# Driver counts, pairwise output transposes and the rank of the norm roots in a hybrid RWKV-7/S5 layer

## The chip, the core and the metric

The kernel runs on one core of a Trainium2 chip. The metric is the device time of one execution in microseconds (us); smaller is better. TensorE is called PE in the profile (PEld is its weight load), VectorE DVE, ScalarE ACT, GpSimd POOL and the SyncE queue SP.

## What is computed

One layer of a decoder trunk on x of 1 x 1024 x 1024 in float32, cut to what matters here:

```python
h = rms_norm(x, norm_mix_pre)
proj = h @ w_in                       # RWKV columns | S5 input u | two gates of 1024
o_rwkv = rwkv7_branch(...) @ w_branch_rwkv
o_s5   = s5_branch(...)    @ w_branch_s5
mixed = (sigmoid(gA) * o_rwkv + sigmoid(gB) * o_s5) @ w_out
x = x + rms_norm(mixed, norm_mix_post)
h = rms_norm(x, norm_ffn_pre)
x = x + rms_norm(conv_ffn(h, ...), norm_ffn_post)

# rwkv7_branch, per head of 64, for each time step t:
S = S * w_t + (S @ a_t) b_t^T + v_t k_t^T ;  y_t = S @ r_t
y = (y - mean) * rsqrt(var + 64e-5) * lnx_w + lnx_b      # per head
y = (y + sum(r * k * r_k) * v) * g
```

## The kernel before

The products are split: each float32 operand is a high part and a low part, and three matmuls of 128x512 stand for one (lines 171 to 175). One such triple is one *filler step*. Time is cut into two halves of 512 positions (`th` 0 and 1), the 512 RWKV channels into four blocks of 128, two per group `g`. The RWKV recurrence is solved in chunks of 64 steps: gram products (line 715), the inverse of triangular 32x32 blocks on DVE (`rwkv_inv`, lines 768 to 798: 30 pairs of multiply and add, in at 776 and out at 792 and 797 through DRAM), a level that joins the 32-blocks (`rwkv_level`, line 800), then eight chained chunks (`rwkv_chain`, line 855). `rwkv_out` (line 899) norms each head on DVE and ACT, transposes the result on PE (line 922), and multiplies it with the factors.

**Who sets PE's order.** PE's instructions stand in the order in which Python traces them. The middle of the kernel is traced by `drive` (lines 185 to 207). It holds *lanes*, generators whose steps yield a tuple of three: PE cost, how long until the lane may go on (or a condition), and optionally a weight. Beside them stands a list of *filler*: dense products, in a fixed order (gate tiles of the input projection, `merge`, `merge_s5`, `outproj`). `drive` has a clock `now` and a `credit`:

```python
if self.fill and self.credit < 0:
    continue                                   # no lane may step
...
self.now += r[0]
self.credit -= PACE * r[0] * (r[2] if len(r) > 2 else 1)      # PACE 0.8
lane[2] = r[1] if callable(r[1]) else self.now + r[1]
```

When no lane is due, or the credit is negative, one filler step is traced; it adds 0.68 to clock and credit, and the credit is capped at 2.0. So a lane step's second number is the planner's due time for the next step, and its cost times weight says how much filler must follow before another lane step. Lanes are tried in the order prep 0, prep 1, chain, output (line 1848). When the lanes are done, `drain` traces filler until `outproj` of half 0 is complete (line 1849); then `mix_out` goes on with `merge_rk`, which needs the split outputs of `rwkv_out` for half 1.

The steps of half 1 that matter:

- `chain_lane` (1878): `rwkv_nat` of group 0 (line 1882; transposes at 746 and 761 into natural layout, copied out by ACT at 753, 755 and 766), one wide piece of PE work with cost 2.0.
- `out_lane` (1893): `rwkv_out` of half 0, first pair due 32.0 (`T_LN`) after the chain of half 0. It takes both blocks of a group at once: eight transposes into two PSUM buffers `rp` (there are two in all), two ACT evictions (926), four DVE operations (934), and on SP four loads (933) and two stores `YR` (939). Two such steps, cost 1.0.
- `prep_lane` 1: the transposes of `kb` (701, two `rp` buffers, read by DVE at 703), two gram steps (715), the load for the inversion, `rwkv_nat` of group 1, then the inversion, which the driver counts as `T_INV` = 43.0 (line 1875) before the level may start.
- `rwkv_level`: block transposes on DVE (811) of what came back from DRAM (`gr`), then PE products (821, 831).
- after the chain of half 1, `rwkv_out` of half 1, first pair due `T_LE` = 20.0 later, factors loaded ahead; its squares lie in the three `ev` buffers (line 911), which the filler's gate loads (1184) use as well.

`merge_load` (1194) loads the four `YR` tiles; it is tried once from `merge_loads`, between two gate tiles of the filler, and does nothing while `outs` is under 2, that is until the output lane of half 0 is through; `merge` calls it again.

**Who sets the order on the other engines.** A list scheduler ranks instructions by priority: `high_priority(HPW)` (400000) for filler and weights, `HP2` (200000) for the prep and chain lanes and the middle norms, `HP` (100000) for the output lane, `HPN` (500000) for the start. Of what it counts as ready, the highest rank goes first; the order that results is fixed.

**Norm roots.** `rstd` (262) is one scaling and `rsqrt` (124): nine dependent small DVE operations, of which the last (139) releases `spread`, four PE transposes (271).

Of the kernel before, what the change touches and what calls it, by code (L numbers as in the profile page):

```python
# [12 lines left out]
AF = mybir.ActivationFunctionType  # L13
ALU = mybir.AluOpType
# [52 lines left out]
class Kern:  # L67
# [194 lines left out]
    def rstd(self, ss, eps, scale):  # L262

        v = self.small.tile([128, 4], F32, tag="rv", name=self.nm("rv"), bufs=2)
        self.nc.vector.tensor_scalar(v, ss[:, :4], scale, eps, ALU.mult, ALU.add)
        return self.rsqrt(v, 4, "nr")

    def spread(self, bc, y):

# [629 lines left out]
    def rwkv_out(self, ds, th, latency):  # L899

        nc, V, G, A = self.nc, self.nc.vector, self.nc.gpsimd, self.nc.scalar
        o = slice(th * 512, th * 512 + 512)
        for g in range(2):
            yn = self.yn[:, g].rearrange("p c u h i -> p (c u h) i")
            mean = self.small.tile([128, 16], F32, tag="lm", name=self.nm("lm"), bufs=2)
            V.tensor_reduce(mean, yn, AX.X, ALU.add)
            V.tensor_scalar(mean, mean, 1.0 / 64, None, ALU.mult)
            V.tensor_tensor(yn, yn, mean.unsqueeze(2).to_broadcast([128, 16, 64]), ALU.subtract)
            var = self.small.tile([128, 16], F32, tag="lv", name=self.nm("lv"), bufs=2)
            for j in range(2):  # L910
                sq = self.ev((128, 8, 64)) if th else self.tg("ld", NLD, (128, 8, 64))
                A.activation(sq, yn[:, 8 * j:8 * j + 8], AF.Square)
                V.tensor_reduce(var[:, 8 * j:8 * j + 8], sq, AX.X, ALU.add)
            V.tensor_scalar(var, var, 1.0 / 64, 64e-5, ALU.mult, ALU.add)
            y = self.rsqrt(var, 16, "or")
            V.tensor_tensor(yn, yn, y.unsqueeze(2).to_broadcast([128, 16, 64]), ALU.mult)
        yield 0, latency
        for g, d in enumerate(ds):
            ps = [self.rp((128, 4, 128)) for u in range(2)]
            for u in range(2):  # L920
                for c in range(4):
                    nc.tensor.transpose(ps[u][:, c], self.yn[:, g, c, u], self.cst("ident"))
            for u in range(2):
                p = 2 * g + u
                y1 = self.tg("ld", NLD)
                A.activation(y1, ps[u].rearrange("p c t -> p (c t)"), AF.Identity, bias=self.vec("lnx_b", p),
                             scale=self.vec("lnx_w", p))
                for src, op in ((d["bv"][u], ALU.add), (self.TG[p][:, o], ALU.mult)):
                    if th:
                        t = self.fac.pop(0)  # L930
                    else:
                        t = self.tg("ld", NLD)
                        nc.sync.dma_start(t, src)
                    V.tensor_tensor(y1, y1, t, op)
                if th:
                    self.brk.append(self.slots("eb", p))
                    self.split(*self.brk[p], y1)
                else:
                    nc.sync.dma_start(self.YR[p], y1)
            yield 1.0, 6.0 if th else 2.5  # L940


    def inproj(self, *jobs):
# [922 lines left out]
    def prep_lane(self, g):  # L1866
        for th in range(2):
            yield 0, (lambda: self.masked >= 2 * th + 1 and self.all_in) if g else (lambda: self.chunks >= 14 * th)
            d = self.ds[th][g]
            self.rwkv_tiles(d, g, th)  # L1870
            yield from self.rwkv_front(d, g, th, self.pts[th], (lambda: self.chains >= 1) if th > g else (lambda: self.grams > 2 * th) if g else T_LD)
            self.fronts += 1
            if g:
                yield from self.rwkv_inv(self.ds[th], th)
                yield 0, T_INV
                self.preps += 1

    def chain_lane(self):
        for th in range(2):
            ds = self.ds[th]  # L1880
            yield 0, lambda: self.fronts >= 2 * th + 1
            self.rwkv_nat(ds[0], 0)
            yield 2.0, lambda: self.preps > th
            yield from self.rwkv_level(ds)
            yield 0, lambda: self.outs >= 2 * th
            yield from self.rwkv_chain(ds, self.pts[th], th)
            if th:
                self.early_stack.close()
                self.early = self.early_stack.enter_context(self.tc.tile_pool(name="early", bufs=1, side="right"))
                self.chained = True  # L1890
            self.chains += 1
# [16 lines left out]
T_LD, T_SQ, T_LT = 6.0, 3.0, 3.5  # L1908
NEVA = 4
T_KN, T_BK, T_GR, T_NF, T_MT, T_INV, T_LV, T_CH = 7.0, 4.0, 4.0, 5.0, 8.0, 43.0, 1.0, 0.8  # L1910
T_LN, T_LE = 32.0, 20.0
T_N0, T_RS, T_N1, T_N2, T_N4, T_N5, T_N3 = 2.5, 4.0, 2.2, 5.0, 1.6, 40.0, 2.0
NET = 5
MGAP = 2
# [17 lines left out]
HPW, HPN = 400000, 500000  # L1932
# [64 lines left out]
```

## Time and profile before

| | us |
|---|---|
| three runs | 1499.52, 1508.82, 1509.49 (median 1508.82) |
| the profiled execution, own time | 1501.13 |
| its span, first to last instruction | 1499.4 |
| PE busy in the span | 1436.3 |
| DVE busy | 1072.2 |
| ACT busy | 730.3 |

Rows of the timeline read: start in us from the span's start, duration, engine, line, operation, output <- inputs, shape, count, and in brackets how long the engine was idle before and what released it. Rows of the waits read: who waited <- for whom: total us, times, longest. Rows of the windows read: stretch, its length, then busy time and instructions of PE, PEld, DVE, ACT and POOL, the granted PE clock (1.00 is full), the DMA share and GB/s.

### The profile page before, as it was taken

The numbers are of one execution on the slowest core, as the hardware profiler recorded it, in microseconds if no ns is written. First come the engines' busy times: TensorE is split into PE (matmuls) and PEld (weight loads), VectorE is DVE, ScalarE is ACT, GpSimd is POOL, SyncE is SP. The second block draws the span as 40 slices with busy tenths as digits, with TensorE's granted clock in tenths as the row PEclk, the third lists the DMA queues.
The fourth block names the chain that finished last, engine by engine and source line by source line (L and its number), as shares of the span: only waits on it lengthen the run. The fifth ranks groups of instructions, "written<-read, shape, count | busy, mean of one in ns | idle before, by whom it ended". The sixth has DMA issues, their size and how long they took to land. (4 is left out here: it accounts for less than half of the span.)

```text
span 1499.4 us, 24150 instructions
## 1 busy us (share of the span) xinstructions
PE 1436.3 (96%) x9284; PEld 1177.0 (78%) x9284; DVE 1072.2 (72%) x1761; ACT 730.3 (49%) x1167; POOL 58.7 (4%) x116
## 2 busy tenths in 40 slices
PE   7999999999999899798999999999999999999996
PEld 5778888788878687576878877888888887888785
DVE  8977774756226859456597799777777777697677
ACT  7677653533324564443455455444444444444351
POOL 0000000010100110100000000000000000000001
PEclk9999999999999999799999999999999999999997
DMA  6453432642512675433365633222222227943723
GB/s 221 124 187 113 131 94 93 203 133 100 170 52 76 189 222 177 135 100 113 117 197 179 204 125 128 84 79 78 83 85 84 85 71 243 322 143 126 229 95 112
DMA packets 121284, 206.26 MB, mean 138 GB/s; under 512 B 29248, under 2 KB 35520, under 8 KB 121168
## 3 DMA queue, kind: packets, MB, share of 16 engines
q1 hardware_dynamic: 113296, 182.43, 37.7%
q0 software_dynamic: 6144, 19.99, 4.0%
q10 hardware_dynamic: 1728, 2.29, 0.4%
q8 instruction: 73, 1.20, 0.3%
q14 instruction: 43, 0.35, 0.1%
HBM read 150.14 MB, written 52.43 MB: 135 GB/s over the span
## 5 line engine op out<-in xcount | busy, mean ns | idle before, releaser
L172 PE MATMUL gm<-hh,wh 128*128 128x512 f32 x672 | 276.6, 412 | 8.0 <-DVE rsy L139 5.1
L173 PE MATMUL gm<-hl,wh 128*128 128x512 f32 x672 | 265.7, 395 | 0.0
L174 PE MATMUL gm<-hh,wl 128*128 128x512 f32 x672 | 265.3, 395 | 0.0
L156 ACT CAST wh<-wf 128x512 fp32r<-128x512 f32 x171 | 105.7, 620 | 186.3 <-PE gm L173 117.8
L157 DVE TENSOR_TENSOR wl<-wf,wh 128x512 fp32r<-128x512 f32 x171 | 117.0, 687 | 91.6 <-ACT wh L156 89.2
L172 PEld LDWEIGHTS gm<-hh,wh 128*128 128x128 f32 x672 | 127.9, 190 | 40.2 <-issue 7.9
L174 PEld LDWEIGHTS gm<-hh,wl 128*128 128x128 f32 x672 | 128.1, 191 | 28.1
L173 PEld LDWEIGHTS gm<-hl,wh 128*128 128x128 f32 x672 | 128.3, 191 | 25.1 <-issue 1.0
L1615 PE MATMUL d<-xl,wh 128*128 128x512 f32 x308 | 120.8, 392 | 3.5 <-DVE xl L227 3.5
L1614 PE MATMUL d<-xh,wh 128*128 128x512 f32 x308 | 120.9, 392 | 2.1 <-ACT xh L226 2.1
L1616 PE MATMUL d<-xh,wl 128*128 128x512 f32 x308 | 120.6, 392 | 0.0
L1440 PE MATMUL rp<-t,h 128*128 128x512 f32 x216 | 84.4, 391 | 2.6 <-ACT p L1454 1.6
L1442 PE MATMUL rp<-t,l 128*128 128x512 f32 x216 | 84.2, 390 | 0.5 <-DVE l L227 0.5
L1441 PE MATMUL rp<-t,h 128*128 128x512 f32 x216 | 84.1, 389 | 0.0
L1615 PEld LDWEIGHTS d<-xl,wh 128*128 128x128 f32 x308 | 58.2, 189 | 16.7 <-DVE xl L227 4.7
L1614 PEld LDWEIGHTS d<-xh,wh 128*128 128x128 f32 x308 | 58.2, 189 | 14.8 <-ACT xh L226 2.5
L1616 PEld LDWEIGHTS d<-xh,wl 128*128 128x128 f32 x308 | 58.1, 189 | 12.1
L226 ACT CAST h<-r 128x1024 fp32r<-128x1024 f32 x34 | 35.8, 1054 | 61.1 <-PE rp L1441 29.6
L227 DVE TENSOR_TENSOR l<-r,h 128x1024 fp32r<-128x1024 f32 x34 | 41.6, 1224 | 29.2 <-ACT h L226 27.7
L1461 DVE SCALAR_TENSOR_TENSOR y<-zv,vecs,y 128x1023 f32<-128x1023 f32 (+1 forms) x36 | 46.1, 1280 | 8.5 <-ACT y L1459 8.5
L1440 PEld LDWEIGHTS rp<-t,h 128*128 128x128 f32 x216 | 40.5, 188 | 12.2 <-ACT p L1454 2.5
L1454 ACT COPY p<-rp 128x512 f32<-128x512 f32 x54 | 31.0, 574 | 37.0 <-PE rp L1442 37.0
(459 smaller groups left out, 3198.5 us busy)
## 6 DMA issues: line engine op xcount, KB each, us to landing
r<-in_w_up_dram SPq DMA_DIRECT2D x36, 512.0 KB, 3.6
wf<-in_w_in_dram SPq DMA_DIRECT2D x62, 256.0 KB, 2.9
st<-in_w_down_dram SPq DMA_DIRECT2D x55, 256.0 KB, 4.1
st<-ACT SPq DMA_DIRECT2D x44, 256.0 KB, 4.4
wf<-in_w_up_dram SPq DMA_DIRECT2D x36, 256.0 KB, 2.6
ACT<-y POOLq DMA_DIRECT2D x18, 512.0 KB, 2.9
GT<-ev SPq DMA_DIRECT2D x32, 256.0 KB, 2.5
wf<-in_w_br_dram SPq DMA_DIRECT2D x32, 256.0 KB, 2.7
```

What stands on the lines that cost most here:

```text
L156: nc.scalar.copy(h[:, :n], f[:, :n])
L157: nc.vector.tensor_tensor(l[:, :n], f[:, :n], h[:, :n].bitcast(F32), ALU.subtract)
L172: mm(ps, a, xh[k], start=k == 0, stop=False)
L173: mm(ps, a, xl[k], start=False, stop=False)
L174: mm(ps, b, xh[k], start=False, stop=k == n - 1)
L1440: mm(ps, wh[:, c], xh, start=first and k == 0, stop=False, skip_group_check=True)
L1441: mm(ps, wh[:, c], xl, start=False, stop=False, skip_group_check=True)
L1442: mm(ps, wl[:, c], xh, start=False, stop=k == 3, skip_group_check=True)
L1461: V.scalar_tensor_tensor(y[:, lag:], z[:, 0:1024 - lag], self.vec(nme, i), y[:, lag:], ALU.mult, ALU.add)
L1614: mm(ps, wh[:, c], xh[:, x], start=start, stop=False, skip_group_check=True)
L1615: mm(ps, wh[:, c], xl[:, x], start=False, stop=False, skip_group_check=True)
L1616: mm(ps, wl[:, c], xh[:, x], start=False, stop=stop, skip_group_check=True)
```

## The change

Five edits, all in how the middle is planned and ranked; no arithmetic and no transfer is added or removed.

```diff
     def rstd(self, ss, eps, scale):
         v = self.small.tile([128, 4], F32, tag="rv", name=self.nm("rv"), bufs=2)
-        self.nc.vector.tensor_scalar(v, ss[:, :4], scale, eps, ALU.mult, ALU.add)
-        return self.rsqrt(v, 4, "nr")
+        with self.tc.high_priority(HPN):
+            self.nc.vector.tensor_scalar(v, ss[:, :4], scale, eps, ALU.mult, ALU.add)
+            return self.rsqrt(v, 4, "nr")
...
         for g, d in enumerate(ds):
-            ps = [self.rp((128, 4, 128)) for u in range(2)]
-            for u in range(2):
-                for c in range(4):
-                    nc.tensor.transpose(ps[u][:, c], self.yn[:, g, c, u], self.cst("ident"))
             for u in range(2):
                 p = 2 * g + u
+                ps = self.rp((128, 4, 128))
+                for c in range(4):
+                    nc.tensor.transpose(ps[:, c], self.yn[:, g, c, u], self.cst("ident"))
                 y1 = self.tg("ld", NLD)
...
-            yield 1.0, 6.0 if th else 2.5
+                yield (0.5, 3.0) if th else (0.5, 1.2, 4)
...
-                yield 0, T_INV
+                yield 0, T_INV2 if th else T_INV
...
-            yield 2.0, lambda: self.preps > th
+            yield 2.0, (lambda: self.preps > th), 2.5
...
-T_LN, T_LE = 32.0, 20.0
+T_LN, T_LE, T_INV2 = 32.0, 16.0, 50.0
```

So: the inversion of half 1 is counted as 50 instead of 43; the natural layouts in the chain lane take 2.5 times their cost from the credit; the output transposes go block by block, in half 0 with weight 4 and 1.2 to the next, in half 1 with 3.0 to the next; the outputs of half 1 are due 16 instead of 20 after the chain; and the operations of the norm roots are traced at rank `HPN`.

More of the change, by code (lines that the diff above doesn't have):

```diff
@@ L918, in rwkv_out @@
         for g, d in enumerate(ds):
-            ps = [self.rp((128, 4, 128)) for u in range(2)]
-            for u in range(2):
-                for c in range(4):
-                    nc.tensor.transpose(ps[u][:, c], self.yn[:, g, c, u], self.cst("ident"))
             for u in range(2):
                 p = 2 * g + u
+                ps = self.rp((128, 4, 128))
+                for c in range(4):
+                    nc.tensor.transpose(ps[:, c], self.yn[:, g, c, u], self.cst("ident"))
                 y1 = self.tg("ld", NLD)
-                A.activation(y1, ps[u].rearrange("p c t -> p (c t)"), AF.Identity, bias=self.vec("lnx_b", p),
+                A.activation(y1, ps.rearrange("p c t -> p (c t)"), AF.Identity, bias=self.vec("lnx_b", p),
                              scale=self.vec("lnx_w", p))
```

## The prediction

> **What bounds the kernel now.** I read the page first, then PE's waits between 300 and 900 us, where every edit but the start's roots lies.
>
> ```profile
> PE 1436.3 (96%) x9284; PEld 1177.0 (78%) x9284; DVE 1072.2 (72%) x1761; ACT 730.3 (49%) x1167; POOL 58.7 (4%) x116
> ```
>
> ```profile
> PE cz L821 <- DVE ld L811: 6.7, 2, 5.1
> PE gm L172 <- DVE rsy L139: 5.1, 1, 5.1
> PE rp L821 <- DVE ld L811: 3.9, 2, 3.6
> PE rp L922 <- ACT ld L926: 2.1, 2, 1.6
> PE rp L271 <- DVE rsy L139: 2.1, 1, 2.1
> PE rp L701 <- DVE bk L703: 1.3, 1, 1.3
> PE rp L922 <- ACT V L766: 1.2, 1, 1.2
> ```
>
> PE is busy 96% and its work does not change; it is only reordered. So the change is worth the PE stops it removes, less those it makes. The seven rows hold 22.4 us: the level (10.6), one stop of the filler (5.1), the output transposes with `kb` behind them (4.6) and one norm root (2.1).
>
> The level costs more than its stops. It is done twice, with the same ten filler steps inside:
>
> ```profile
> 391.21 0.60 PE L761 MATMUL rp<-csts,ld 128*128 128x128 f32 x4
> ...
> 396.94 1.20 PE L821 MATMUL cz<-ld,gr 32*32 32x32 f32 x64
> 397.97 1.18 PE L821 MATMUL rp<-ld,gr 32*32 32x32 f32 x64
> ...
> 404.95 0.69 PE L873 MATMUL cz<-S,ar 64*64 64x64 f32 x32
> ```
>
> ```profile
> 593.86 0.60 PE L761 MATMUL rp<-csts,ld 128*128 128x128 f32 x4
> ...
> 604.79 0.28 PE L821 MATMUL cz<-ld,gr 32*32 32x32 f32 x2 [5.13 <-DVE ld L811]
> ...
> 623.66 0.69 PE L873 MATMUL cz<-S,ar 64*64 64x64 f32 x32
> ```
>
> From the first transpose (761) to the chain (873) half 0 takes 13.74 us, half 1 29.80: 16.06 more. The stops of half 1 are 10.3 of it (6.7 and 3.6 in the waits); the rest is the clock, seen in windows of 2 us:
>
> ```profile
> 602.00:604.00 2.00, 0.00 (x0) 0.00 (x0) 0.31 (x2) 1.71 (x3) 1.75 (x4) 0.72 0.51 142
> 604.00:606.00 2.00, 0.28 (x2) 0.18 (x2) 1.97 (x4) 0.00 (x0) 1.73 (x3) 0.50 1.09 212
> ...
> 620.00:622.00 2.00, 2.00 (x42) 1.75 (x39) 0.69 (x1) 1.92 (x6) 0.00 (x0) 0.50 0.75 254
> ```
>
> PE went idle at 599.66 (604.79 less 5.13). A mean of 0.72 over 602 to 604 is full clock until 602.9, then half: it fell 3.2 us into the idleness, and was still half at 622.
>
> **The driver's count, before and after.** A filler step is 0.68 in the driver, and on the chip too (eleven steps in 7.48 us):
>
> ```profile
> 383.05 0.39 PE L172 MATMUL gm<-hh,wh 128*128 128x512 f32 x1
> ...
> 390.53 0.39 PE L172 MATMUL gm<-hh,wh 128*128 128x512 f32 x1
> ```
>
> So a count of steps is a count of time. I set the clock to 0 at half 1's `rwkv_nat`. The credit there is 1.96: cap 2.00, less 0.72 for line 697, plus one step. The output lane is already due, `kb` at 6.32.
>
> Before: nat 0 to 2.0, credit 0.36; pairs of group 0 to 3.0; 4 fillers; pairs of group 1 at 5.72; `kb` 6.72; 3 fillers; out lane done 9.66; first gram 11.70; second gram 17.98; second nat 34.58; level 80.10.
>
> After: nat takes 4.0 credit (2.0 x 0.8 x 2.5), leaving -2.04: 3 fillers; pair 0 at 4.04 takes 1.6; 3 fillers; `kb` 6.58; 1 filler; pair 1 at 8.16; 2 fillers; pair 2 at 10.02; 3 fillers; first gram 12.56; 2 fillers; pair 3 at 16.12; 3 fillers; out lane done 18.66; second gram 19.34; second nat 35.94 to 37.94; then 74 fillers where 64 stood (50 for 43); level 88.26.
>
> So the level comes 8.16 later by count, 12 filler steps, 6.80 of it measured from the second gram, where the inversion's data leave. The same weight on half 0's nat changes nothing: seven fillers follow there anyway, because `kb` is not due. No filler is lost: at the end of the output lane 18 steps of `outproj` (12.2 us) are left to `drain`, before it was 26.
>
> **The level.** What the inversion delivers, against the second gram:
>
> ```profile
> 529.20 1.98 PE L715 MATMUL cz<-ar,bk 64*64 64x128 f32 x64
> ```
>
> ```profile
> 600.29 1.98 POOL L797 DMA_DIRECT2D gr<-xd  x3 [4.78 <-DMA xd<-mt]
> 602.51 3.22 POOL L797 DMA_DIRECT2D gr<-xd  x5 [0.24 <-issue]
> ```
>
> ```profile
> gr<-xd POOLq DMA_DIRECT2D x8, 64.0 KB, 3.9
> ```
>
> ```profile
> 603.94 0.70 DVE L811 STREAM_TRANSPOSE ld<-gr 32x512 f32<-32x512 f32 x1 [1.69 <-DMA gr<-xd]
> ```
>
> The first 761 now comes at 593.86 - 529.20 + 6.80 = 71.46 after the gram. By half 0's rows PE wants the first `L821` 5.73 later, at 77.2, and those of group 1 6.76 later, at 78.2. Group 0's transposes can start at 74.74 and take 1.4: in time. The last `gr` load is issued at 605.1 and lands 3.9 later, at 79.8; two transposes: 81.2. PE waits 3.0 there instead of 10.3, too short for the clock to fall as it did. Gain 16.06 - 3.0 = 13.1. Bounds: all of it hidden, 16.1; or the transposes stay queued on DVE behind filler splits, the stop passes 3.2 us and the clock falls: about 11 left, gain 5.
>
> The price: 12 more steps of `merge` run without lane work between them. Each tile there needs `ev` buffers for a gate load and, at four tiles, for an S5 load, and there are three. What such a shortage costs shows once, below (7.2 us); I allow 2.0, between 0 and 7.2, near the low end because the waits show no stop of that kind at the merge tiles before the level: no row of `L172` but the one of 5.1 is among the longest.
>
> **The output transposes of half 0.**
>
> ```profile
> 502.87 1.91 PE L746 MATMUL cz<-csts,bk 128*128 128x128 f32 x8
> ...
> 507.67 0.60 PE L922 MATMUL rp<-csts,mt 128*128 128x128 f32 x4
> ```
>
> ```profile
> 506.00:508.00 2.00, 2.00 (x15) 2.00 (x13) 1.58 (x3) 1.64 (x6) 0.00 (x0) 0.67 0.24 90
> ```
>
> ```profile
> 513.58 0.78 ACT L926 ACTIVATE ld<-rp,vecs 128x512 f32<-128x512 f32 x1
> ```
>
> Nat takes 4.8 us on the chip, not 2.0, in part because the clock is half until 507.3 (a mean of 0.67 over 506 to 508). ACT copies its results until 513.58; only then is the first pair taken out and its `rp` freed, at 514.36. The stops there sum to 4.6.
>
> The clock comes back while nothing but transposes runs (502.87 to 507.67), and so before the first pair; I count nothing for the fillers put there. The Trainium skill (TensorE: Matmul & The Clock Gate, "Part 4: PE-mode transpose") says that transposes do not count as activity for the clock. By that rule the fillers between nat and the first pair would bring the clock back, and the first pair would run at full speed, about 0.3 us more gained than in the sum; by the row, which disagrees, nothing.
>
> After: pair 0 at 507.67 + 2.04 = 509.7, `kb` at 512.2 takes the other `rp`, its second half needs pair 0's and waits from 512.7 to 514.4: 1.7. Later pairs find their buffer free. Gain 2.9; bounds 0 to 4.6. Moved with the pairs, each with two loads and a store on SP: the last `YR` store is 9 us later, so `merge_loads` (eight fillers after nat) finds `outs` 0 and does nothing; the four `YR` loads move to `merge`, 40 fillers after nat (eight, and the 32 of the last gate tiles), some 20 us after the last store. That cover hides them; if it went, PE would stop once at the head of `merge`, some 7 us by the stop below. On POOL the clearing of `mt` waits for the last pair, which reads that buffer; it ends 2.7 before the second gram starts, and nothing on POOL is due before that gram.
>
> **The outputs of half 1.**
>
> ```profile
> 684.88 1.22 DVE L906 TENSOR_REDUCE lm<-mt 128x16 f32<-128x1024 f32 x1
> ...
> 696.67 0.68 DVE L1192 SCALAR_TENSOR_TENSOR hl<-ev,gm 128x512 f32<-128x512 f32 x1
> ...
> 699.62 1.22 DVE L916 TENSOR_TENSOR mt<-mt,rsy 128x1024 f32<-128x1024 f32 x1
> ```
>
> ```profile
> 692.14 0.33 SPq L1184 DMA_DIRECT2D ev<-GT  x1
> ```
>
> ```profile
> 697.50 0.77 PE L172 MATMUL gm<-hh,wh 128*128 128x512 f32 x1 [5.06 <-DVE rsy L139]
> ...
> 701.90 0.40 PE L173 MATMUL gm<-hl,wh 128*128 128x512 f32 x1
> ```
>
> The row blames line 139, but what frees `gm` is the gate (1192) at 696.67, whose load could be issued only at 692.14: the squares of the head norm hold `ev` buffers. Then ten matmuls take 4.40 instead of 2.27. The stop is worth 5.06 + 2.1 = 7.2. After, the chain ends 12 steps later in the filler; before, ten steps of `merge_s5` were left there. So `outproj` runs there, whose `gm` ACT copies out without a gate load: this stop goes. The first pair, 24 steps or 16.3 us after the chain, meets outputs that now need 16.0 us for both groups (684.88 to 700.84): I allow 1.0 for lateness. Gain 6.2, bounds 0 and 7.2.
>
> **The roots.**
>
> ```profile
> 749.67 0.16 DVE L265 TENSOR_SCALAR rv<-rp 128x4 f32<-128x4 f32 x1
> ...
> 756.65 0.65 PE L271 MATMUL rp<-csts,rsy 128*128 128x128 f32 x4 [2.09 <-DVE rsy L139]
> ```
>
> ```profile
> 30.15 0.15 DVE L137 TENSOR_TENSOR rsh<-rsy 128x4 f32<-128x4 f32 x1
> 30.22 0.74 DVE L982 SCALAR_TENSOR_TENSOR hl<-x,vecs,hh 128x512 fp32r<-128x512 f32 x1
> 30.89 0.15 DVE L138 SCALAR_TENSOR_TENSOR rsh<-rsh,rv 128x4 f32<-128x4 f32 x1
> ```
>
> The start's root already has rank `HPN`, and still a wide operation stands between each two of its small ones, 0.74 a step: the next small one is not ready when DVE falls free. So rank takes out only the runs of several wide ones. Of this root's 7.0 us I take 1.1 off; bounds 0 and 2.1. The other roots stop PE by nothing that rank can change.
>
> **The sum.** 13.1 - 2.0 + 2.9 + 6.2 + 1.1 = 21.3, from the profiled execution's own 1501.13: 1479.8. That execution lies 1.6 above the lowest run and 7.7 below the median of 1508.82, and its span is 1499.4 of it; a stop removed shortens both alike. So a median of a few runs may lie up to 7.7 above such a sum; I take half, 3.8, and predict 1484.
>
> **Rivals.** First, the level's stop is halved but stays long enough for the clock (for it: DVE is busy 1.97 of the 2.0 us from 604 on, so its transposes queue with filler work; against it: 6.8 us of new distance): gain 5 there, 3 at the outputs, the rest as above, less 2.0: 10, so 1491 to 1495. Second, the counts do what they say but the stops return as shortage of `ev` in the filler, two stops of 7.2 beside a hidden level: 16.1 + 2.9 + 6.2 + 1.1 - 14.4 = 11.9, so 1489 to 1493. Third, on the other side, that same shortage at all four merge tiles with an S5 load: 28.8 against 26.3 gained, 2.5 slower, 1504 to 1508; it decides from 3.7 such stops. For it: three `ev` and two loads a tile; against it: before the level the filler ran through such tiles unstopped. More than 1% slower needs six such stops.
>
> **How the numbers follow.** Forecast 0.60, first rival 0.20, second 0.12, third 0.08. A difference under 1% (15 us) is about what a measurement of this kernel cannot tell from none. Faster by over 1%: most of the forecast, 0.58. Slower by over 1%: 0.05, the far part of the third. The rest, 0.37, is within 1%. The range takes the forecast's bounds (a gain near 30 is 1471) and both middle rivals with the spread of runs, up to 1503.
>
> **What would show it.** Right: no wait of `L821` over 4 us, clock 1.00 through the level, no stop of `L172` at the outputs of half 1, three or four fillers between nat and the first pair, `spread` of half 0's first middle root stopping PE by about 1. Wrong: new waits of `L172` on gates (1192) before the level; `L821` still late; a stop at the head of `merge`; outputs of half 1 waited for by PE.

## The result, and the profile after

The kernel after takes 1490.26 us (median of 4 runs, 1486.72 to 1492.89) beside 1505.70 of the kernel before (median of 4, 1499.52 to 1509.49): ratio 0.9902, 95% interval 0.9873 to 0.9930, so 1.0% less. A second measurement of it among the experiments gave 0.9924 (0.9907 to 0.9940). The two profiled executions are 1501.13 and 1492.89, 8.2 apart: that of before lies 4.6 below its median, that of after 2.6 above, so the traces show about half of what the medians do. A second profile of the kernel after (after_again below) ends at 1492.99, so it too shows 8.1.

PE's busy time, from the first part of the page of after, is the same to 0.5 us; the work was only reordered:

```profile
PE 1435.8 (96%) x9284; PEld 1176.3 (79%) x9284; DVE 1071.2 (72%) x1761; ACT 729.8 (49%) x1167; POOL 58.9 (4%) x116
```

PE's longest waits between 300 and 900 us, after (total, times, longest):

```profile
PE gm L172 <- DVE ev L1192: 4.3, 2, 3.0
PE gm L172 <- ACT ev L1147: 4.2, 2, 2.7
PE rp L702 <- ACT ld L926: 2.2, 1, 2.2
PE rp L822 <- ACT hh L231: 2.0, 1, 2.0
PE rp L272 <- DVE rsy L139: 1.4, 1, 1.4
```

The level's 10.6 (now line 822) has become 2.0 and small pieces, and the filler's 5.1 at the outputs of half 1 is gone. In their place the filler itself waits 8.5, on the evictions of the last gate tiles (1147) and on the gates of `merge` (1192). PE's timeline shows where:

```profile
529.03 1.98 PE L716 MATMUL cz<-ar,bk 64*64 64x128 f32 x64
...
543.95 0.50 PE L172 MATMUL gm<-hh,wh 128*128 128x512 f32 x1 [1.48 <-ACT ev L1147]
...
557.34 0.79 PE L172 MATMUL gm<-hh,wh 128*128 128x512 f32 x1 [2.70 <-ACT ev L1147]
...
607.17 0.47 PE L172 MATMUL gm<-hh,wh 128*128 128x512 f32 x1 [3.04 <-DVE ev L1192]
...
611.58 0.60 PE L762 MATMUL rp<-csts,ld 128*128 128x128 f32 x4
...
616.24 0.47 PE L172 MATMUL gm<-hh,wh 128*128 128x512 f32 x1 [1.30 <-DVE ev L1192]
...
622.64 0.28 PE L822 MATMUL rp<-ld,gr 32*32 32x32 f32 x2 [2.03 <-ACT hh L231]
623.28 1.91 PE L822 MATMUL rp<-ld,gr 32*32 32x32 f32 x62 [0.36 <-DVE ld L812]
...
631.83 0.69 PE L874 MATMUL cz<-S,ar 64*64 64x64 f32 x32
```

The stretches between such marks, with the filler steps that the driver moved (0.68 us each) taken out, give the account. The steps between the marks were counted in the traces. The last column but one reads after_again in the same way.

| stretch of PE | before | after | steps moved in | gain | gain in after_again | predicted |
|---|---|---|---|---|---|---|
| start to half 1's nat | 502.87 | 504.65 | 0 | -1.8 | 0.0 | 0 |
| nat to second gram | 26.33 | 24.38 | 2 | 3.3 | 3.3 | 2.9 |
| second gram to level | 64.66 | 82.55 | 10 | -11.1 | -7.8 | -2.0 |
| level to chain | 29.80 | 20.25 | 0 | 9.6 | 6.4 | 13.1 |
| chain to half 0's `spread` | 132.99 | 116.45 | -12 | 8.4 | 8.4 | 7.3 |
| `spread` to end | 742.7 | 742.8 | 0 | -0.1 | -2.1 | 0 |

The third row is the one that missed. It is made of the stops of 1.48, 2.70 and 3.04, less one of 0.81 that before has there, and of half clock from 556.62 to 563.45 and from 607.82 to 611.24, which costs half of the time that PE is busy in it (3.1 and 1.7): 11.2. The windows over the two (PE's busy time stands first, the granted clock, 0.50, behind POOL's):

```profile
556.62:563.45 6.83, 6.11 (x14) 4.79 (x15) 5.39 (x14) 4.42 (x10) 0.00 (x0) 0.50 0.57 173
...
607.82:611.24 3.42, 3.42 (x10) 2.67 (x9) 1.70 (x3) 1.58 (x3) 3.17 (x6) 0.50 0.97 214
```

The third and the fourth row belong together: what the filler loses ahead of the level gives the inversion's data time to arrive, so the level then stops for less. The two profiles of the same program divide the loss differently and have the same sum, -1.5 and -1.4, where 11.1 was predicted.

### The profile page after: what moved, and what is told of

Its sections match the earlier page's. It is cut to its first block, busy times and chain, and to the rows that moved or that the text cites. A ratio compares the mean times of both kernels' runs of the same rounds, so it can differ in the third digit from the quotient of the medians.

```text
span 1491.1 us, 24155 instructions
## 1 busy us (share of the span) xinstructions
PE 1435.8 (96%) x9284; PEld 1176.3 (79%) x9284; DVE 1071.2 (72%) x1761; ACT 729.8 (49%) x1167; POOL 58.9 (4%) x116
## 5 line engine op out<-in xcount | busy, mean ns | idle before, releaser
L1440 PEld LDWEIGHTS rp<-t,h 128*128 128x128 f32 x216 | 40.5, 188 | 11.2 <-ACT p L1454 2.5
```

The source lines that it names most:

```text
L1440: mm(ps, wh[:, c], xh, start=first and k == 0, stop=False, skip_group_check=True)
```

## The experiments

Two theories stood at first. A: the output pairs, spread over 14 us, bring the last inputs of `merge` late, and that stops the filler at the gate tiles and starts the inversion late. B: the longer count itself has that price. Each run was timed six to twelve times beside the kernel before (after itself four times). For the table each profile is read like the one above: first the ratio, then what the stretch from half 1's nat to the first chain step gains over before, then the stretch from there to `spread`, each with the moved steps (column two) taken out.

| run | steps moved ahead of the chain | ratio (95%) | nat to chain | chain to `spread` |
|---|---|---|---|---|
| after | 12 | 0.9902 (0.9873 to 0.9930) | 1.8 | 8.4 |
| after_again | 12 | 0.9924 (0.9907 to 0.9940) | 1.9 | 8.4 |
| count_only | 10 | 0.9942 (0.9919 to 0.9965) | 0.1 | 7.6 |
| pairs_only | 2 | 0.9988 (0.9972 to 1.0005) | -1.8 | -3.4 |
| weights_undone | 11 | 0.9936 (0.9911 to 0.9961) | 2.7 | 8.5 |
| s5_in_ld | 12 | 0.9927 (0.9902 to 0.9952) | -2.8 | 8.4 |
| s5_inputs_later | 12 | 0.9945 (0.9927 to 0.9962) | -2.0 | 8.3 |
| ties_on_dve | 12 | 0.9911 (0.9894 to 0.9927) | 6.8 | 8.3 |
| later_and_ties | 12 | 0.9933 (0.9913 to 0.9952) | 0.7 | 8.3 |
| count_58 | 24 | 0.9951 (0.9934 to 0.9968) | -1.9 | 6.9 |
| s5_tiles_earlier | 12 | 0.9914 (0.9894 to 0.9935) | 0.4 | 7.3 |
| ties_and_ld | 12 | 0.9940 (0.9921 to 0.9958) | 3.4 | 8.3 |
| level_distance | 18 | 0.9946 (0.9926 to 0.9965) | 3.5 | 8.3 |

The last column is steady: about 8 us wherever the count is 50 or more, a loss where it is 43. The one ahead of it wanders between -2.8 and 6.8 whatever was edited. The two outer stretches, start to nat and `spread` to end, add -2.6 to 0.6 and -4.0 to 4.5, and differ between after and after_again, one program, by 1.8 and 2.0; that is part of why the ratios do not follow the two columns.

**count_only** (against before):

```diff
-T_LN, T_LE = 32.0, 20.0
+T_LN, T_LE, T_INV2 = 32.0, 20.0, 50.0
-                yield 0, T_INV
+                yield 0, T_INV2 if th else T_INV
```

> The kernel before with the count of half 1 alone raised to 50 (pairs, weights, ranks as before). Two theories of why the change gave less than the sum. Theory A (late inputs): the output pairs of half 0, spread over 14 us instead of 6, bring the rows of YR and so the S5 inputs of merge late; their GELUs then stand on ScalarE between the last gate tiles' copies and the second nat's; the filler stops there (1.48 and 2.70 in the profile after, with the clock down to half) and the copy with which the inversion begins (line 782) comes 4.4 us later. Theory B (the count's own price): the longer count itself makes those stops, since it puts merge tiles where no lane work stands between them, and three ev buffers don't carry them. A expects here: no filler stop over 1 us within 12 us behind the second nat, the inversion's store at 48 to 49 us behind that nat as before, the level stopped by less than 1 us, one filler stop of about 3 us at the merge tiles with an S5 load, and the stop of 5.06 at the outputs of half 1 gone: level 16 less 3 to 6, plus 7, so 17 to 20 us gained, ratio 0.987 to 0.989. B expects the gate-tile stops here too, and a gain no better than that of the whole change: 0.991 to 0.994.

No stop at the gate tiles, and the stop at the outputs of half 1 is gone: so far A. But the ratio, 0.9942, is not A's 0.987 to 0.989, as the level, said to be hidden, takes 25.1 us, for a reason in neither theory. Its rows on GpSimd, ScalarE, VectorE and PE:

```profile
604.38 3.22 POOL L797 DMA_DIRECT2D gr<-xd  x5 [0.25 <-issue]
```

```profile
611.92 1.13 ACT L1167 ACTIVATE ld<-ev 128x512 f32<-128x512 f32 x1 [2.54 <-DMA ev<-YU]
...
614.52 0.23 ACT L809 COPY ld<-rp 128x2 f32<-128x2 f32 x2
```

```profile
613.08 0.69 DVE L1192 SCALAR_TENSOR_TENSOR ev<-ev,gm 128x512 f32<-128x512 f32 x1 [2.63 <-DMA ev<-GT]
...
616.69 0.69 DVE L811 STREAM_TRANSPOSE ld<-gr 32x512 f32<-32x512 f32 x1
```

```profile
617.53 0.22 PE L821 MATMUL cz<-ld,gr 32*32 32x32 f32 x2 [5.04 <-DVE ld L811]
...
620.25 1.86 PE L821 MATMUL cz<-ld,gr 32*32 32x32 f32 x61 [2.50 <-DVE ld L811]
```

The data are issued by 607.6 (604.38 and 3.22) and land a median of 5.3 us behind their issue, yet the first transpose runs at 616.69. It must follow a small copy (809) into the same tile, which stands on ScalarE behind a GELU that waited 2.54 us for an S5 load; VectorE's queue ahead of it waited 2.63 for a gate load. So the level's own small steps are queued behind filler that waits for loads. The Trainium skill (Perfetto Trace Analysis, "Tensor Engine Instruction (MATMUL, LD_WEIGHTS)") calls the queues of these two engines strictly first in, first out; these rows agree.

**pairs_only** (the change with the count at 43, `T_LE` 20 and no rank for the roots):

```diff
-T_LN, T_LE, T_INV2 = 32.0, 16.0, 50.0
+T_LN, T_LE, T_INV2 = 32.0, 20.0, 43.0
-        with self.tc.high_priority(HPN):
-            self.nc.vector.tensor_scalar(v, ss[:, :4], scale, eps, ALU.mult, ALU.add)
-            return self.rsqrt(v, 4, "nr")
+        self.nc.vector.tensor_scalar(v, ss[:, :4], scale, eps, ALU.mult, ALU.add)
+        return self.rsqrt(v, 4, "nr")
```

> The kernel before with the output transposes pair by pair and their weights alone (count 43, rank and T_LE as before). Theory A expects the stops at the gate tiles (together about 4 us, with half clock behind the longer one), the inversion's store about 4 us later behind the second nat, so the level stopped for 7 to 12 us and at half clock, and the stop at the outputs of half 1 still there, as the count is what removes it: 3 gained at the first pairs, 7 lost at the gate tiles, a little back at the level: ratio 0.998 to 1.004. Theory B expects the 3 us gained at the pairs to stay: 0.996 to 0.998, with no stop at the gate tiles.

PE's two filler stops:

```profile
545.76 0.50 PE L172 MATMUL gm<-hh,wh 128*128 128x512 f32 x1 [4.05 <-ACT ev L1146]
...
701.75 0.77 PE L172 MATMUL gm<-hh,wh 128*128 128x512 f32 x1 [7.11 <-DVE hl L1191]
```

The gate-tile stop is there without the count, and the stop at the outputs of half 1 stays without it. With count_only this splits the two: the pairs' spread makes the first, the count removes the second. The time agrees with A, though B's 0.998 lies in its interval too. One part of A missed: the inversion's store, said to come 4 us later behind the second nat, came 48.6 behind it, as in before (48.4); it was that nat itself that came 6.0 later behind the second gram. The stop's link to the spread holds throughout: in all eleven profiles here with the pairs spread the filler waits for that eviction (1146 or 1147), 1.5 to 6.6 us in total; in before, count_only and weights_undone it has no such wait.

**weights_undone** (after, with the two weights taken out):

```diff
-            yield 2.0, (lambda: self.preps > th), 2.5
+            yield 2.0, (lambda: self.preps > th), 1.0
-                yield (0.5, 3.0) if th else (0.5, 1.2, 4)
+                yield (0.5, 3.0) if th else (0.5, 1.2, 1)
```

> The kernel after with the two weights undone (nat 2.5 to 1, pairs of half 0 4 to 1): still pair by pair, still the count of 50, but by the driver's count the four pairs are done 7.8 after the nat instead of 18.7 and merge_loads finds them done. Theory A expects the stops at the gate tiles to fall below 1 us, the inversion's store at 48 to 49 us behind the second nat instead of 53, the level's stop of 2.0 gone: 7 to 10 us faster than the kernel after, ratio to before 0.983 to 0.986. Theory B expects the time of the kernel after, 0.989 to 0.991.

The stops at the gate tiles are gone, as A said; the 7 to 10 us are not gained. Closer together the pairs wait again for their `rp`:

```profile
516.76 0.66 PE L924 MATMUL rp<-csts,mt 128*128 128x128 f32 x4 [3.46 <-ACT ld L926]
```

From nat to the second gram this kernel needs 28.38 us for 17 steps, after 24.38 for 18. One stop stands for the other. The level's stop of 2.0, which A had gone, is there too: line 822 waits 3.7, the longest 2.2.

**s5_in_ld** (after):

```diff
-        self.ys5.append(self.s5_y(self.ev((128, 8, 64)), b, 1, self.tg("ld", NLD)))
+        self.ys5.append(self.s5_y(self.tg("ld", NLD, (128, 8, 64)), b, 1, self.tg("ld", NLD)))
```

> The kernel after with the four S5 loads of merge (line 1247) put into an ld buffer instead of an ev buffer; nothing is left out. Both theories expect the filler's stops of 3.04 and 1.30 at the merge tiles to go or to halve, as the gate loads no longer wait for ev. Theory B (the shortage is a price of its own): 4 to 6 us faster than after, ratio 0.986 to 0.987. Theory A with a fixed arrival of the inversion's data: the level is only reached that much earlier and waits that much longer, so the stops move from the filler to lines 812 and 822 and the time stays within 1.5 us of after, 0.989 to 0.991.

The merge tiles' stops fall from 4.3 to one of 1.24, so most of them were the shortage of `ev`. But the gate tiles stop for longer, and the inversion's data leave 7 us later than in after (601.12 there):

```profile
545.37 0.50 PE L172 MATMUL gm<-hh,wh 128*128 128x512 f32 x1 [2.79 <-ACT ev L1147]
...
561.52 0.79 PE L172 MATMUL gm<-hh,wh 128*128 128x512 f32 x1 [3.84 <-ACT ev L1147]
```

```profile
608.27 0.55 POOL L793 DMA_DIRECT2D xd<-mt  x1 [58.33 <-DVE mt L791]
```

The edit doesn't touch the gate tiles; the same stops are 4.2 in after and 2.4 in after_again, which are one program. At line 822 the level's stops rose from 2.7 in after to 6.0, as A had said. Neither theory is settled by its time.

**after_again** (no edit) measures that spread.

> The kernel after, unchanged, as the base for the three runs beside it. Expected: 0.990 of before, within 0.988 to 0.993, with the filler's stops at the gate tiles (1 to 4 us, in one or two pieces), at the merge tiles with an S5 load (about 3 and 1) and the level at 20 to 23 us from its first transpose to the chain.

As expected, at the upper end of the band.

**s5_inputs_later** (after):

```diff
-MGAP = 2
+MGAP = 4
-            if i < 2:
-                inputs((2 * i, 2 * i + 1))
+            if i in (2, 3):
+                inputs((2 * i - 4, 2 * i - 3))
```

> The kernel after with the S5 inputs of half 0 taken up two merge tiles later (i in 2, 3 instead of 0, 1; MGAP 4 instead of 2, so the four GLU tiles move two places too); pairs, weights and count as after. It separates what the pairs' spread does from the way it does it. Theory A (ScalarE's order: the GELUs that wait for late S5 inputs stand in front of the last gate tiles' copies) expects the stops at the gate tiles under 1 us with the pairs still spread, the inversion's first copy (line 783) at most 4 us behind the second nat instead of 6.4, and 3 to 8 us off the kernel after, less where the level then waits. Rival (the late pairs hurt through the queue of SP or through ev buffers, whatever ScalarE's order is): the stops stay above 2 us together and the time stays within 1.5 us of after.

The edit didn't make the case that it was to test. On ScalarE the GELU (1167) still runs ahead of the gate tile's eviction (1147), as in after, though it now stands two tiles later in the program:

```profile
542.90 1.12 ACT L1167 ACTIVATE hh<-ld 128x512 f32<-128x512 f32 x1
543.82 0.64 ACT L1147 ACTIVATE ev<-gm,hb_b_gate 128x512 f32<-128x512 f32 x1
```

The stop is 2.67 and the time 3 us over after_again. A's first copy of the inversion did come earlier, 3.8 behind the second nat, and its store 45.6 behind it (53.0 in after, 48.6 in after_again); the level still took 23.4, so the earlier inversion did not shorten it here. That ScalarE's order makes the gate tiles' stop is read from the rows of after below; no run here changed it alone.

```profile
539.26 1.33 ACT L226 CAST hh<-ld 128x512 fp32r<-128x512 f32 x2 [3.42 <-DMA ld<-YR]
541.04 1.28 ACT L1167 ACT_TABLE_LOAD   x1 [0.44 <-DMA ld<-YU]
542.34 1.12 ACT L1167 ACTIVATE hh<-ld 128x512 f32<-128x512 f32 x1
543.25 0.64 ACT L1147 ACTIVATE ev<-gm,hb_b_gate 128x512 f32<-128x512 f32 x1
```

The eviction that PE waits for until 543.95 follows casts that waited 3.42 us for the last `YR` rows, a table load and a GELU. SyncE's last loads of these rows, in before and in after:

```profile
530.36 2.26 SPq L1199 DMA_DIRECT2D ld<-YR  x3
```

```profile
536.43 0.93 SPq L1199 DMA_DIRECT2D ld<-YR  x2
```

In after SyncE waited up to 3.4 us for the last `YR` stores to land (536.4 and 537.0) and then issued these loads at once, with the four loads of S5 inputs (1166) behind them in its queue.

**ties_on_dve** (after):

```diff
-            self.nc.scalar.copy(x2[:, 0, 1:2], tie[:, 0, 0:1])
+            V.tensor_copy(x2[:, 0, 1:2], tie[:, 0, 0:1])
-            A.copy(xz[:, :, 0, 0:1], tie[:, 0:2, 0:1])
+            V.tensor_copy(xz[:, :, 0, 0:1], tie[:, 0:2, 0:1])
```

> The kernel after with the two small copies that start the inversion (line 783) and the level's transposes (line 810) on VectorE instead of ScalarE; nothing is left out. In the profiles so far they stand 3.7 to 7.7 us behind the second nat and 2.3 to 8.5 us behind the level's first transposes, behind GELUs and casts of the filler. Theory A2 (ScalarE's queue sets when the inversion starts and when the level's transposes may run) expects the first to come within 2.5 us behind nat, the inversion's store as much earlier, and the level 2 to 5 us shorter: 3 to 7 us faster than after, ratio to before 0.985 to 0.988. Rival (the scatter of the inversion's data and VectorE's own queue set it): the inversion starts earlier but the time stays within 1.5 us of after.

The inversion's copy came 5.0 behind nat, not 2.5 (549.35 to the row below). The level took 20.1, as in after (20.2; 23.4 in after_again), without a stop over 1 us at line 822 but with one of 2.26 in the filler inside it. The ratio is 0.0013 under after_again's and the intervals overlap: a gain is not shown.

```profile
554.39 0.16 DVE L783 COPY mt<-rp 128x1 f32<-128x1 f32 x1 [2.13 <-issue]
```

**later_and_ties** has both edits.

> Both edits of the two runs before it in the kernel after. If A and A2 both hold the gains add in part, as both bring the inversion's start forward and the level can only be hidden once: 7 to 11 us faster than after, ratio to before 0.983 to 0.986. If neither: the time of after.

0.9933: neither gain.

**count_58** (after):

```diff
-T_LN, T_LE, T_INV2 = 32.0, 16.0, 50.0
+T_LN, T_LE, T_INV2 = 32.0, 16.0, 58.0
```

> The kernel after with the count of half 1 at 58 instead of 50: twelve more filler steps, three merge tiles, between the second nat and the level. Theory D: the level still takes 20 to 23 us (half 0: 13.7) although the inversion's data are there, because its small copies and transposes queue on ScalarE and VectorE behind the merge tiles with an S5 load, which wait for their own loads. With 58 these tiles lie ahead of the level. D expects the level at 14 to 17 us with no stop over 1 us and full clock, the stops of 3 and 2 at the merge tiles as before, and 3 to 6 us less than the kernel after: ratio to before 0.986 to 0.989. Rival E (distance is used up, and what the level waits for lies on its own path): level at 19 us or more, time within 1.5 us of after.

D falls. The data were issued by 608.2 (first fence), the merge tiles lie behind, and the level still takes 21.4 us:

```profile
604.94 3.22 POOL L798 DMA_DIRECT2D gr<-xd  x5 [0.25 <-issue]
```

```profile
619.91 0.60 PE L762 MATMUL rp<-csts,ld 128*128 128x128 f32 x4
...
627.47 0.22 PE L822 MATMUL cz<-ld,gr 32*32 32x32 f32 x2 [1.16 <-DVE ld L812]
628.12 1.19 PE L822 MATMUL cz<-ld,gr 32*32 32x32 f32 x62 [0.43 <-DVE ld L812]
...
630.18 1.91 PE L822 MATMUL rp<-ld,gr 32*32 32x32 f32 x62 [0.42 <-DVE ld L812]
...
641.29 1.13 PE L874 MATMUL cz<-S,ar 64*64 64x64 f32 x32
```

What is left is the level's own way, from PE over ScalarE's copies and VectorE's transposes back to PE: 7.6 us from the first row to the second, where half 0 took 5.7. Small stops follow, and half clock with them from 629.8 on. Of the 7.6 us by which this level is longer than half 0's, 2.0 are stops at line 822 and 5.6 half clock (half of the time that PE was busy in it). So E is right on the level; its time is not shown, as 0.9951 is 4 us over after_again, with intervals that overlap.

**s5_tiles_earlier** (after):

```diff
-            if 2 <= m < 6:
-                self.s5_inputs(m - 2)
+            if m < 4:
+                self.s5_inputs(m)
```

> The kernel after with the four S5 loads of merge two tiles earlier (m 0 to 3 instead of 2 to 5), count 50. It moves the same tiles out of the level from the other side. Theory D expects the level at 14 to 17 us without stops over 1 us, the stops of the merge tiles now 5 us earlier and no larger than 3 and 2, and 3 to 6 us less than after: 0.986 to 0.989. Rival E: level at 19 or more, time within 1.5 us of after. A third way: the stops of the merge tiles vanish as well, because the loads no longer meet the scatter of the inversion's data, and 6 to 9 us are gained.

E holds: level 23.9, stops at the merge tiles 2.04 and 1.60, and 0.9914, within 1.5 us of after_again by the ratio.

**ties_and_ld** puts the edits of ties_on_dve and s5_in_ld together.

> The kernel after with both small copies on VectorE (as in ties_on_dve) and the S5 loads in ld buffers (as in s5_in_ld). If the stops at the merge tiles are the shortage of ev, they fall from 4.8 us together to under 2 here and 2 to 4 us are gained over ties_on_dve: ratio to before 0.988 to 0.990. If their loads are late whatever buffer they take, the stops stay and the time is that of ties_on_dve, 0.991.

The merge tiles' stop is 1.08 and no more, so again it was `ev`; the time did not follow (0.9940). As in s5_in_ld the inversion became slower: from its first copy to its store 48.5 and 49.4 us in these two, 41.8 to 46.5 in all the others. That filler and inversion take VectorE from each other would explain it; it is argued, not shown.

**level_distance** (after):

```diff
-        yield 0.4, T_LT
+        yield 0.4, T_LT if ds is self.ds[0] else T_LT2
-T_LD, T_SQ, T_LT = 6.0, 3.0, 3.5
+T_LD, T_SQ, T_LT, T_LT2 = 6.0, 3.0, 3.5, 8.0
```

> The kernel after with one more distance inside the level of half 1: between its first transposes (line 762) and its first small matmuls (822) the driver counts 8.0 instead of 3.5, twelve filler steps instead of six; the count ahead of the level stays 50. With 58 the data lay ready 8 us before the level began and the level still took 21.4 us, with idle pieces of 1.16, 0.43, 0.23 and 0.42 at line 822 and half clock behind them: the way from the first transposes over ScalarE's copies and VectorE's transposes back to TensorE is longer (7 to 8 us) than the 4.1 us of filler that cover it. Theory F (that way is what is left of the level's excess): no stop at line 822 over 0.5 us, full clock through the level, first transpose to chain 17 to 19 us with 4.1 of them more filler, so 5 to 7 us less than after: ratio to before 0.984 to 0.988. Rival G (ScalarE and VectorE are given the more work ahead of the transposes the more filler runs there): the transposes come as much later, the level takes 23 to 26 us, the time is within 1.5 us of after.

F falls, and G fits better. The level takes 26.3 us, 22.2 without the added steps, with stops of 1.07 and 1.06 at line 822; the time is 3 us over after_again, not within 1.5. The last two transposes came as much later, each behind a filler split on VectorE; the last:

```profile
625.56 0.64 DVE L232 SCALAR_TENSOR_TENSOR hl<-ev,hh 128x512 fp32r<-128x512 f32 x1
626.23 0.70 DVE L812 STREAM_TRANSPOSE ld<-gr 32x512 f32<-32x512 f32 x1
```

No version here is faster than the kernel after beyond its interval.

## Why the prediction was right, and where its sum was wrong

The sign and the range were right: 1490.3 and 1491.8 against 1484, between 1471 and 1503. The range was wide, though, and held both middle rivals with it. The sum of 21.3 was not right: the traces show 8.3 and 8.2. Of the signs that the prediction named, the stop at the outputs of half 1 went and no wait of the level was over 4 us, but the clock did not stay at 1.00 through the level, and a sign of being wrong came: waits on the gates (1192) before the level. By its steps:

- **The outputs of half 1 and the root: right.** Predicted 6.2 and 1.1. The last stretch but one gained 8.4: 7.8 up to the first pair (709.59 - 631.83 = 77.76, was 89.60, less 4.08 of moved steps) and 0.6 at the root. The stop of 7.2 went whole; the 1.0 set aside for late outputs was not needed. count_only and pairs_only show that the count did it. The root's stop fell from 2.09 to 1.35, 0.7 where 1.1 stood; it is 1.35 or 1.36 in ten of the eleven profiles with the new rank (2.03 in count_58) and 2.08 in count_only and pairs_only, which have the old one.

```profile
709.59 0.60 PE L924 MATMUL rp<-csts,mt 128*128 128x128 f32 x4
...
748.28 0.65 PE L272 MATMUL rp<-csts,rsy 128*128 128x128 f32 x4 [1.35 <-DVE rsy L139]
```

- **The output transposes of half 0: right**, 3.3 for 2.9 in both profiles of after; the nine others with the pairs spread show 1.7 to 2.0. `kb` waits 2.2 where 1.7 was predicted (line 702 in the waits above). The rule on transposes that the prediction weighed fails here too: the same four transposes take 1.06 and then 0.60. The granted clock is half until 508.84, and in the 3.4 us before that PE ran nothing but these transposes; in before it came back at 507.33 in the same way.

```profile
504.65 1.91 PE L747 MATMUL cz<-csts,bk 128*128 128x128 f32 x8
506.35 1.06 PE L762 MATMUL rp<-csts,ld 128*128 128x128 f32 x4
507.20 1.84 PE L747 MATMUL cz<-csts,bk 128*128 128x128 f32 x8
508.88 0.60 PE L762 MATMUL rp<-csts,ld 128*128 128x128 f32 x4
```

- **The level: mechanism partly right, size wrong.** 9.6 and 6.4 for 13.1. The stop was put at 3.0; line 822 waits 2.7 in after, and the filler inside another 1.30. But this is no test of the 3.0: the level began 82.55 us after the second gram, where 71.46 was counted, and the last of the inversion's data landed at 87.2 (616.2 on the clock of the trace), where 79.8 was counted. Not foreseen was that the clock falls all the same (1.91 for 62 small matmuls where half 0 took 1.18 for 64). The deeper error shows in count_58 and level_distance: the bound of "all of it hidden, 16.1" was not to be had by any distance tried (8.4 and 7.6). The prediction timed the data's arrival and half 0's path; in half 1 that path runs through ScalarE and VectorE while `merge` fills both.
- **The price of 2.0: the step that failed.** It measured 11.1 in after and 7.8 in after_again. Two parts, told apart by the runs. The merge tiles' `ev` shortage (3.04, with 1.7 of half clock) is the one allowed for, and count_only has it too (2.3). The other, 1.48 and 2.70 with 3.1 of half clock, comes from the spread of the pairs; it is 2.41 with 1.7 of half clock in after_again. The prediction had seen that the `YR` loads move, had costed it at nothing under "that cover hides them", and had put 7 us on it if the cover went, at the head of `merge`. There was no such cover. It counted 20 us of filler on PE between the last store and the loads; but SyncE issued the loads 0.02 us after the stores had landed, and ScalarE ran the casts that read them ahead of the last gate tiles' evictions. So the stop is not at the reader of the rows, it is at the gate tiles whose evictions share ScalarE with it. Both middle rivals (gains of 10 and 11.9) were nearer to the 8.3 than the forecast, the second, stops back as shortage in the filler, in its mechanism too.
- **Median and profile.** 3.8 was added for the spread of runs, and the medians came out on the other side: the gain between medians (15.4; 11.8 in the second measurement) is larger than between profiles. That the time came within 6.3 us of 1484 with a sum 13 us too high is luck: the profile of before lay low among its runs and that of after high.

What stays open: why nat to chain comes out so nearly the same. Taken over all edits with a count of 50 or more it gained -2.8 to 6.8, in the middle about 1, against 14.0 predicted (2.9 - 2.0 + 13.1). What the gains are made of can be read: PE is idle there for 16.0 us in before and 10.8 to 17.9 in the others, and half clock costs 8.8 in before and 5.0 to 11.8 in the others; the two together give each gain within 1.4 us. Most stops that an edit removed were matched by others in the same stretch. With one profile of the kernel before, and terms that differ by 3.3 us between two profiles of one program, single terms under some 3.5 us there are not settled.

## What to carry to other kernels

Before a stop is booked as gain, name the queues that its work passes through, not only the time at which its data arrive: a small copy in the order of an engine that the filler also uses can be as late as the filler's latest load. A delay put between pieces of work moves every later reader of their results, and the stop may appear at a bystander that shares an engine with that reader. When several edits of one stretch all leave its sum where it was, look for the gain in another stretch; here it lay where the longer count had changed which filler ran beside the outputs.

## What the runs showed of the clock

The prediction took 3.2 us of idleness as the point where the clock falls. The granted clock shows another rule: within each of the fourteen profiles it changes only at points that lie whole multiples of 3.413 us apart, to within 3 ns. In after it is half from 502.01 to 508.84, from 556.62 to 563.45, from 607.82 to 611.24 and from 621.48 to 628.30. The 602.9 of the prediction is such a point, and the 3.2 only its distance from the start of that stop. In one kernel, after_again, a stop of 2.41 us was followed by half clock and a longer one of 3.14 was not. The two stops, and the windows between such points:

```profile
543.13 0.50 PE L172 MATMUL gm<-hh,wh 128*128 128x512 f32 x1 [2.41 <-ACT ev L1147]
...
603.71 0.47 PE L172 MATMUL gm<-hh,wh 128*128 128x512 f32 x1 [3.14 <-DVE ev L1192]
```

```profile
540.97:544.38 3.41, 1.25 (x5) 1.05 (x6) 0.00 (x0) 3.40 (x5) 0.02 (x1) 1.00 0.97 233
544.38:547.79 3.41, 3.41 (x9) 2.64 (x8) 1.39 (x2) 3.41 (x6) 0.55 (x1) 0.50 0.62 187
...
599.00:602.41 3.41, 1.56 (x7) 0.95 (x6) 1.23 (x2) 1.97 (x3) 0.00 (x0) 1.00 1.01 316
602.41:605.82 3.41, 2.11 (x9) 1.80 (x10) 2.17 (x4) 1.94 (x3) 2.76 (x5) 1.00 0.83 221
```

The first stop lies almost whole in one window, which leaves PE 1.25 us of work, and the next window is at half clock; the second is divided between two, which keep 1.56 and 2.11. Between 300 and 900 us of the fourteen profiles, every full-clock window of filler alone in which PE was busy for up to 0.42 of the time was followed by half clock (18 windows), and none with 0.43 or more. Among the level's small matmuls less idleness was enough: in count_58 the clock fell at 629.81 behind a window with 1.62 of 3.41 us busy (0.47), and it stayed at half from 633.23 to 640.05 although PE was busy throughout, with the level's matmuls and some filler. So the length of one stop does not decide, and the same stop can cost 1.7 us (half of a window) or more on top, or nothing, by where it falls. The Trainium skill (TensorE: Matmul & The Clock Gate, "Part 1: The HAM clock gate") says that activity is judged in a free-running window of about 3.4 us; these rows agree with that.
